# Reordering the last expert sets and moving the final norm's roots in a one-core transformer layer

## The chip, the cores and the metric

The kernel runs on one core of a Trainium2 chip. The metric is the device time of one execution in microseconds. TensorE (PE) multiplies, VectorE (DVE) and ScalarE (ACT) do elementwise work, GpSimd (POOL) issues the gathers and does small elementwise work, SyncE (SP) issues plain transfers. Each engine runs its own instructions in program order and waits for others by semaphores.

## The reference

One layer over 256 latent tokens of width 2048: an adaLN-modulated RMSNorm, a mixer (mLSTM and differential attention), a gated residual, and then the part that matters here, a PEER block (each token and head retrieves its best 16 of 16384 single-neuron experts), a second gated residual and a final RMSNorm:

```
def block(args):
    hx, ix, gx = args
    act = jax.nn.gelu(jnp.einsum('td,ted->te', hx, expert_u[ix]), approximate=False)
    return jnp.einsum('te,ted->td', (gx * act), expert_v[ix])
...
x = x + g2 * peer(...)
return rmsnorm(x, final_norm_w)      # x * rsqrt(mean(x*x) + EPS) * w
```

## The kernel before, in words

The 256 tokens are two tiles of 128 (tile 0 and tile 1). Everything up to the second einsum is left as it is by the change; what follows concerns the end, where gathered rows of expert_v are multiplied into the output.

**Blocks and items.** Lists of experts are cut into blocks of 128 rows. For each block POOL issues two gathers on its software queue, in this order: `ag` (gates and activations, L1548 to L1554, 128 columns for a block of a set, 256 for one of a whole tile, 512 for a block that serves both tiles) and `vraw` (128 rows of expert_v, 2048 floats each, 1 MB, L1528). `ITEMS` (L83) is the written-out order of the work. An item is one of:

- a *set*: four blocks of one tile, one for each group of 32 tokens. Each matmul is 128 rows by 32 tokens; 16 instructions in all (four blocks by four column chunks `c` of 512).
- a *pair set* (`PAIRS`): four blocks, each serving 32 tokens of tile 0 and 32 of tile 1, so 32 instructions: first all of tile 0, then all of tile 1.
- a *block of a whole tile* or of both tiles: raw rows are split by ACT (`hi`, L1559) and DVE (`lo`, L1561) into two float32r halves and multiplied in three passes, 12 matmuls for each tile that it serves.

In `ITEMS` of before the four pair sets are spread among the blocks of whole and both tiles; behind the fourth pair set come four such blocks and then three sets: `SETS[0][5]` (tile 0), `SETS[1][4]` and `SETS[1][5]` (tile 1). The last twelve blocks are therefore sets.

**Buffers.** `stage_rows` takes row buffers from a ring of six tiles of two rows each (L1510). A gather of `vraw` thus reuses the buffer of the block twelve before it, and has to wait until the matmuls (or splits) that read that block and its neighbour in the two-row tile are through. `fetch` (L1595) issues gathers up to this depth.

**The end** (L1794 on). `v_groups(t, item, parts, cs, last)` (L1620) multiplies an item into tile t's four accumulators `v`, chunk by chunk. `residual(t, c)` (L1797) multiplies the accumulator by the gate `g2` into `yf`, adds to `x` (both DVE), and squares with a sum on ACT into `s4`. For tile 1 and c < 2, POOL multiplies `x` by the final weight `fw` at L1804. `finish_tile(t)` (L1806) sums `s4`, makes the inverse root in `rstd` (DVE L208, then POOL's power L210), scales the four chunks by root and weight (DVE L1816; for tile 1, c < 2, ACT L1814) and stores them, on ACT's queue for c < 2 and on SP's for the rest. `item_weights` makes the 32-column weights `w` of an item on DVE (L1579) from its `ag`. Instructions marked `line` (DVE) and gathers keep the order in which the program writes them; the scheduler places others.

In before, tile 0 ends with the third item from the end; its residual is written in two halves around the weights of the last item, and its `finish_tile` follows the multiplications of the last item but one.

Of the kernel before, what the change touches and what calls it, by code (L numbers as in the profile page):

```python
# [19 lines left out]
F32 = mybir.dt.float32  # L20
# [5 lines left out]
AF = mybir.ActivationFunctionType  # L26
OP = mybir.AluOpType
# [4 lines left out]
P = 128  # L32
D = 2048
# [3 lines left out]
EPS = 1e-6  # L37
# [19 lines left out]
CAPS = (6,) * 8 + (8, 8, 16) + (1,) * 16  # L57
GOES = {0: ((4, EARLY), (1, LATER), (1, N_LIST)), 4: ((4, EARLY), (2, N_LIST))}
BASE = tuple(sum(CAPS[:i]) for i in range(len(CAPS)))
BOTH, PAIR, DENSE = 10, 11, 27  # L60
# [4 lines left out]
def group(kind, t):  # L65
    return kind % 4 if kind < 8 else ((kind - PAIR) % 4 + t * ((kind - PAIR) // 4)) % 4
# [7 lines left out]
def spread(*groups):  # L74
    return [x for _, _, x in sorted(((i + 0.5) / len(g), j, x) for j, g in enumerate(groups) for i, x in enumerate(g))]
# [4 lines left out]
SETS = [[[(4 * t + j, i) for j in range(4)] for i in range(6)] for t in range(2)]  # L80
SOON = [SETS[0][0], SETS[1][0], SETS[0][1], SETS[1][1]] + SETS[0][2:5]
PAIRS = [[(PAIR + 4 * d + g, 0) for g in range(4)] for d in range(4)]
ITEMS = SETS[1][2:4] + [[(DENSE, i)] for i in range(N_LIST, P)] + spread(  # L83
    PAIRS, [[(BOTH, i)] for i in range(CAPS[BOTH])], [[(8 + n % 2, n // 2)] for n in range(16)]) + [
    SETS[0][5], SETS[1][4], SETS[1][5]]


def build(tc, a, dump=None):
    nc = tc.nc
# [3 lines left out]
    def mp_(*args, **kw):  # L93
        tc.keep_in_program_order(mm(*args, **kw))  # L94
# [21 lines left out]
    def load(src, pool, bufs, queue=nc.sync):  # L116
        r = pool.tile([P, 1024], F32, name="raw", tag="raw", bufs=bufs)
        d = queue.dma_start(r, src)  # L118
        if by_four[0]:
            tc.keep_in_program_order(d)  # L120
        return r
# [7 lines left out]
    def line(i):  # L129
        if in_line[0]:  # L130
            tc.keep_in_program_order(i)
# [74 lines left out]
    def rstd(pool, ss, n, w, name):  # L206
        v = pool.tile([P, w], F32, name=name + "v", bufs=1)
        nc.vector.tensor_scalar(v, ss, 1.0 / n, EPS, op0=OP.mult, op1=OP.add)  # L208
        r = pool.tile([P, w], F32, name=name, bufs=1)
        nc.gpsimd.tensor_tensor(r, v, mhalf[:, :w], op=OP.pow)  # L210
        return r
# [221 lines left out]
    for k in range(KT):  # L433
# [7 lines left out]
        for kp in range(4):  # L441
            w = load(a["w_mod1"][k, kp], stx, MOD_BUFS)
# [661 lines left out]
    for k in range(KT):  # L1104
        x = rp.tile([P, T], F32, name="xk", tag="xk", bufs=3)
# [3 lines left out]
                                       op0=OP.add, op1=OP.subtract)  # L1109
# [388 lines left out]
    n = P - N_LIST + 1  # L1498
# [105 lines left out]
    def item_weights(n):  # L1604
        return [(raw, weights_of(kind, ins)) for (kind, _), (raw, ins) in
                zip(ITEMS[n], [fetched.pop(0) for _ in ITEMS[n]])]

    coming = []
# [11 lines left out]
    def v_groups(t, item, parts, cs=range(4), first=False, last=False, into=None):  # L1620
        for c in cs:
            for (kind, _), (raw, ins) in zip(item, parts):
                q = 32 * group(kind, t)
                mp_((into or out_acc[t][c])[q:q + 32, :], lhsT=ins[t], rhs=raw[:, c * 512:(c + 1) * 512],
                    start=first, stop=last, skip_group_check=True)


    x1 = [[None] * 4 for _ in range(2)]
# [75 lines left out]
    for i1 in range(0, P, 2):  # L1704
# [3 lines left out]
        act = act_tail if i1 == N_LIST else gm.tile([P, 2, T], F32, name="act", tag="act", bufs=2)  # L1708
        u_pair(act, pace)
        if i1 == N_LIST:  # L1710
            fetch(0)
            parts = item_weights(0)
        nc.scalar.activation(act, act, AF.Gelu)
        if i1 < N_LIST:
            rows = ag_dram[P + i1 * P:P + (i1 + 2) * P].rearrange("(i p) (t c) -> p i t c", p=P, t=2)
# [51 lines left out]
    with tc.If(rest > 0):  # L1767
        with tc.For_i(0, N_LIST, 1) as i:
            col_ = av.tile([P, 1], F32, name="ocol", bufs=1)
            nc.sync.dma_start(col_, over_dram[:, bass.ds(i, 1)])  # L1770
            for t in range(2):
# [3 lines left out]
                w = ag[:, :, 0]  # L1775
# [13 lines left out]
    N_LAST = len(ITEMS) - 3  # L1789
# [3 lines left out]

    fn = tc.alloc_tile_pool(name="fn", bufs=1, reuse_waits="tile")  # L1794
    s4 = fn.tile([P, 2, 5], F32, name="s4")

    def residual(t, c):  # L1797
        x = x1[t][c]
        y = gm.tile([P, 2, T], F32, name="yf", tag="act", bufs=2).rearrange("p a b -> p (a b)")
        line(nc.vector.tensor_tensor(y, out_acc[t][c], g2[c], op=OP.mult))  # L1800
        line(nc.vector.tensor_tensor(x, x, y, op=OP.add))  # L1801
        nc.scalar.activation(y, x, AF.Square, accum_out=s4[:, t, c:c + 1])  # L1802
        if t and c < 2:
            nc.gpsimd.tensor_tensor(x, x, fw[c // 2][:, c % 2 * 512:c % 2 * 512 + 512], op=OP.mult)  # L1804

    def finish_tile(t):  # L1806
        line(nc.vector.reduce_sum(s4[:, t, 4:5], s4[:, t, 0:4], axis=AX.X))
        r = rstd(fn, s4[:, t, 4:5], D, 1, f"rf{t}")
        rows = a["out"][t * P:(t + 1) * P, :]
        for c in (2, 0, 3, 1):  # L1810
            w = slice(c * 512, (c + 1) * 512)
            x = x1[t][c]
            if t and c < 2:
                nc.scalar.activation(x, x, AF.Copy, scale=r)  # L1814
            else:
                line(nc.vector.scalar_tensor_tensor(x, x, r, fw[c // 2][:, c % 2 * 512:c % 2 * 512 + 512],  # L1816
                                                    op0=OP.mult, op1=OP.mult))
            (nc.scalar if c < 2 else nc.sync).dma_start(rows[:, w], x)


    fnw = a["final_norm_w"]
    fw = [stg.tile([P, 1024], F32, name="fw", tag="raw", bufs=3) for _ in range(2)]
# [1 line left out]
        nc.sync.dma_start(fw[i], bass.AP(tensor=fnw.tensor, offset=fnw.offset + i * 1024, ap=[[0, P], [1, 1024]]))  # L1824
    fetch(N_LAST)
    coming.append(item_weights(N_LAST + 1))
    v_groups(0, ITEMS[N_LAST], coming.pop(0), last=True)
    for c in range(2):
        residual(0, c)
    coming.append(item_weights(N_LAST + 2))  # L1830
    for c in range(2, 4):
        residual(0, c)
    v_groups(1, ITEMS[N_LAST + 1], coming.pop(0))
    finish_tile(0)
    last = coming.pop()
    for c in range(4):
        v_groups(1, ITEMS[N_LAST + 2], last, (c,), last=True)
        residual(1, c)
    finish_tile(1)
    for p in (fn, vex, *v_pools, av, res, gates, vst, tkr, gm, stg, cst, dr):  # L1840
        p.release()

# [68 lines left out]
```

## Time and profile before

| what | us |
|---|---|
| median of 3 runs | 2252.41 |
| lowest and highest | 2245.99, 2253.37 |
| the profiled execution | 2240.84 |
| its span in the profile | 2239.1 |
| PE busy in the span | 2146.8 (96%) |
| DVE, ACT, POOL busy | 1536.1, 1022.1, 784.5 |

A timeline row reads: start and duration in us, engine, line, operation, output <- input, shapes, how many, and in brackets the idle time of that engine before it with what ended it. A row of windows gives, for a stretch of the span, each engine's busy time with its count, the clock granted to TensorE, the DMA engines' mean busy share and what they moved. Line numbers are those of the kernel before.

### The profile page before, as it was taken

The page shows a single profiled execution, that of the slowest core. Times are in us where ns is not written, and L with a number is a line of the kernel's source. Part 1 is how long each engine was busy: PE and PEld are TensorE (multiplying, and loading weights), DVE is VectorE, ACT ScalarE, POOL GpSimd, SP SyncE. Part 2 cuts the span into 40 slices and gives each one's busy share as a digit, 9 for nine tenths or more (in the row PEclk, how much of TensorE's full clock was granted, in tenths as well). Part 3 has the DMA queues.
Part 4 walks back from the last instruction along what each step waited for, and adds up shares of the span by engine and source line. Part 5 has one row for each costly group of instructions (what it writes and reads, how often), then busy time and mean ns, then how long its engine had stood idle before and what let it go on. Part 6 is the DMA issues. An engine that isn't in the chain of part 4 may idle for free. (4 is left out here: it accounts for less than half of the span.)

```text
span 2239.1 us, 37163 instructions
## 1 busy us (share of the span) xinstructions
PE 2146.8 (96%) x14098; PEld 1860.9 (83%) x14098; DVE 1536.1 (69%) x2781; ACT 1022.1 (46%) x1634; POOL 784.5 (35%) x799
## 2 busy tenths in 40 slices
PE   6999999999999999998999999998999999999996
PEld 3668998999899899987998888897888877786773
DVE  3438794566987786855679967777989644544664
ACT  3222232224465854444444678883446333333552
POOL 2122210225554321000223667781221323416763
PEclk9999999999999999999999999999999999999998
DMA  9958883776654678875556568888665798989995
GB/s 379 368 172 310 317 298 96 272 260 195 166 167 131 191 252 279 284 251 179 183 170 193 187 187 236 227 221 235 210 201 183 296 331 332 356 327 380 413 406 226
DMA packets 235845, 563.63 MB, mean 252 GB/s; under 512 B 85218, under 2 KB 118803, under 8 KB 222096
## 3 DMA queue, kind: packets, MB, share of 16 engines
q1 hardware_dynamic: 155328, 339.34, 46.1%
q0 software_dynamic: 45488, 204.33, 25.2%
q10 hardware_dynamic: 34848, 17.57, 2.7%
q8 instruction: 111, 1.82, 0.3%
q14 instruction: 70, 0.57, 0.1%
HBM read 516.99 MB, written 38.93 MB: 248 GB/s over the span
## 5 line engine op out<-in xcount | busy, mean ns | idle before, releaser
L140 ACT CAST hi<-raw 128x1024 fp32r<-128x1024 f32 x528 | 553.2, 1049 | 849.5 <-PE acc L300 275.3
L143 DVE TENSOR_TENSOR lo<-raw,hi 128x1024 fp32r<-128x1024 f32 x476 | 602.4, 1269 | 376.5 <-ACT hi L140 341.3
L94 PE MATMUL s<-h,hi 128*128 128x512 f32 x2048 | 529.1, 400 | 14.5 <-ACT hi L140 13.7
L94 PEld LDWEIGHTS s<-h,hi 128*128 128x128 f32 x2048 | 369.6, 190 | 93.4 <-ACT hi L140 19.3
L300 PE MATMUL acc<-hL,hi 128*128 128x256 f32 x2048 | 333.5, 284 | 0.0
L94 PEld LDWEIGHTS s<-h,lo 128*128 128x128 f32 x2048 | 280.3, 191 | 30.0 <-DVE lo L143 5.5
L300 PEld LDWEIGHTS acc<-hL,hi 128*128 128x128 f32 x2048 | 292.6, 192 | 1.8 <-ACT kA L677 0.3
L94 PE MATMUL s<-h,lo 128*128 128x256 f32 x2048 | 287.1, 283 | 6.9 <-DVE lo L143 3.8
L143 POOL TENSOR_TENSOR lo<-raw,hi 128x1024 fp32r<-128x1024 f32 x52 | 133.6, 2570 | 305.2 <-ACT hi L140 256.7
L300 PE MATMUL acc<-hL,lo 128*128 128x256 f32 x1024 | 175.7, 284 | 0.9 <-DVE lo L143 0.9
L533 DVE SCALAR_TENSOR_TENSOR raw<-raw,cr 128x1024 f32<-128x1024 f32 x128 | 156.3, 1234 | 21.3 <-DMA raw<-w_mod 17.3
L118 POOL DMA_DIRECT2D raw<-w_mod x128 | 67.9, 530 | 289.9 <-DVE raw L533 276.4
L1261 POOL TENSOR_SCALAR o<-iota,i1T,gT 128x128 f32<-128x128 f32 x128 | 147.5, 1160 | 56.4 <-PE g L94 27.9
L1532 POOL DMA_INDIRECT vraw<-expert_v,idxV x96 | 101.5, 1057 | 167.5 <-PE v L94 83.5
L300 PEld LDWEIGHTS acc<-hL,lo 128*128 128x128 f32 x1024 | 150.0, 192 | 2.2 <-DVE lo L143 1.3
L1532 POOL DMA_INDIRECT ag<-ag_dram,idxG x96 | 109.9, 1145 | 79.7 <-DMA ag_dram<-act 37.4
L1561 DVE TENSOR_TENSOR lo<-vraw,hi 128x1024 fp32r<-128x1024 f32 x68 | 82.9, 1225 | 68.4 <-ACT hi L1559 68.2
L300 PE MATMUL acc<-hC,hi 128*128 128x256 f32 x512 | 124.7, 283 | 0.0
L1244 DVE TENSOR_REDUCE act<-s 128x256 f32<-128x512 f32 x126 | 86.1, 684 | 51.0 <-PE s L94 47.4
L94 PE MATMUL v<-hi,l 128*128 128x512 f32 x416 | 114.5, 397 | 0.1
L1559 ACT CAST hi<-vraw 128x1024 fp32r<-128x1024 f32 x68 | 70.8, 1049 | 79.7 <-PE v L94 62.7
L300 PEld LDWEIGHTS acc<-hC,hi 128*128 128x128 f32 x512 | 98.3, 192 | 0.0
(440 smaller groups left out, 3313.4 us busy)
## 6 DMA issues: line engine op xcount, KB each, us to landing
raw<-expert_u SPq DMA_DIRECT2D x256, 512.0 KB, 4.2
raw<-w_in SPq DMA_DIRECT2D x176, 512.0 KB, 4.5
raw<-w_mod POOLq DMA_DIRECT2D x128, 512.0 KB, 5.5
raw<-w_mod SPq DMA_DIRECT2D x64, 512.0 KB, 8.6
raw<-w_out SPq DMA_DIRECT2D x32, 512.0 KB, 4.3
raw<-w_pq SPq DMA_DIRECT2D x32, 512.0 KB, 3.4
ag_dram<-gates SPq DMA_DIRECT2D x32, 512.0 KB, 6.2
ag_dram<-act ACTq DMA_DIRECT2D x126, 128.0 KB, 4.6
```

Of the source, the lines that this page charges most:

```text
L94: tc.keep_in_program_order(mm(*args, **kw))
L118: d = queue.dma_start(r, src)
L140: nc.scalar.copy(h, r)
L143: (nc.vector if shared[0] else nc.gpsimd).tensor_tensor(l, r, h.bitcast(F32), op=OP.subtract)
L300: mm(acc[c][:, g * T:(g + 1) * T], lhsT=hl[sb][:, k2 * 512 + c * P:k2 * 512 + (c + 1) * P], rhs=rhs(sa, g, k), start=first and k2 == 0 and ...
L533: product = nc.vector.scalar_tensor_tensor(r, r, 1.0, cr, op0=OP.mult, op1=OP.mult, accum_out=part[:, h, i:i + 1])
L1244: line(nc.vector.reduce_sum(act[:, e], ps.rearrange("p s t -> p t s"), axis=AX.X))
L1261: (nc.gpsimd if i % 2 else nc.vector).tensor_scalar(o2[:, i], iota, cols[:, i:i + 1], factor[:, i:i + 1], op0=OP.is_equal, op1=OP.mult)
L1532: tc.keep_in_program_order(nc.gpsimd.indirect_dma_start(out=out, out_offset=None, in_=src, in_offset=bass.IndirectOffsetOnAxis(ap=idx[:, b ...
L1559: nc.scalar.copy(h, raw)
L1561: nc.vector.tensor_tensor(l, raw, h.bitcast(F32), op=OP.subtract)
```

## The change

It does four things. In `ITEMS` the fourth pair set and `SETS[0][5]` change places: the set takes the pair set's place among the items, and the pair set is third from the end, so that it is the last item of tile 0. The inverse root is made by ACT (`Sqrt`, with `eps` as bias tile) and DVE (`reciprocal`) instead of DVE and POOL; a `Sqrt` on `eps` into `first` stands ahead of it, behind ACT's last split. POOL's two multiplications by `fw` (L1804) become two on DVE (L1852 in the kernel after), written behind tile 1's last residual. And the order at the end is written anew: tile 0's residual in one piece and its scaling behind the weights of the last item; all four stores of tile 0 on SP; tile 1's chunks 0, 1 scaled and stored by ACT in turn with 2, 3 by DVE and SP.

```
 ITEMS = SETS[1][2:4] + [[(DENSE, i)] for i in range(N_LIST, P)] + spread(
-    PAIRS, [[(BOTH, i)] for i in range(CAPS[BOTH])], [[(8 + n % 2, n // 2)] for n in range(16)]) + [
-    SETS[0][5], SETS[1][4], SETS[1][5]]
+    PAIRS[:3] + [SETS[0][5]], [[(BOTH, i)] for i in range(CAPS[BOTH])], [[(8 + n % 2, n // 2)] for n in range(16)]) + [
+    PAIRS[3], SETS[1][4], SETS[1][5]]
...
+    eps = fn.tile([P, 1], F32, name="eps")
+    nc.vector.memset(eps, EPS)
...
+    on_act(nc.scalar.activation(first, eps, AF.Sqrt))
...
-        nc.scalar.activation(y, x, AF.Square, accum_out=s4[:, t, c:c + 1])
-        if t and c < 2:
-            nc.gpsimd.tensor_tensor(x, x, fw[c // 2][:, c % 2 * 512:c % 2 * 512 + 512], op=OP.mult)
+        on_act(nc.scalar.activation(y, x, AF.Square, accum_out=s4[:, t, c:c + 1]))
...
-        r = rstd(fn, s4[:, t, 4:5], D, 1, f"rf{t}")
...
+        r = fn.tile([P, 1], F32, name=f"rf{t}")
+        on_act(nc.scalar.activation(r, s4[:, t, 4:5], AF.Sqrt, bias=eps, scale=1.0 / D))
+        line(nc.vector.reciprocal(r, r))
+        return r
...
-    v_groups(0, ITEMS[N_LAST], coming.pop(0), last=True)
-    for c in range(2):
+    parts = coming.pop(0)
+    v_groups(0, ITEMS[N_LAST], parts, last=True)
+    v_groups(1, ITEMS[N_LAST], parts)
+    for c in range(4):
         residual(0, c)
     coming.append(item_weights(N_LAST + 2))
-    for c in range(2, 4):
-        residual(0, c)
     v_groups(1, ITEMS[N_LAST + 1], coming.pop(0))
-    finish_tile(0)
+    r = root(0)
+    for c in range(4):
+        scaled(0, c, r)
     last = coming.pop()
     for c in range(4):
         v_groups(1, ITEMS[N_LAST + 2], last, (c,), last=True)
         residual(1, c)
-    finish_tile(1)
+    for c in range(2):
+        line(nc.vector.tensor_tensor(x1[1][c], x1[1][c], fw_of(c), op=OP.mult))
+    r = root(1)
+    for c in range(2):
+        scaled(1, c, r, act=True)
+        scaled(1, c + 2, r)
```

What moves on the engines is shown at three places. The first is POOL's queue where the fourth pair set's gathers stood. Before:

```order
L1532 DMA ag_21962<-ag_dram_83,idxG_10953 128x512
L1532 DMA vraw_21964<-expert_v,idxV_10952 128x2048
L1532 DMA ag_21966<-ag_dram_83,idxG_10953 128x512
L1532 DMA vraw_21964<-expert_v,idxV_10952 128x2048
L1532 DMA ag_21969<-ag_dram_83,idxG_10953 128x512
L1532 DMA vraw_21971<-expert_v,idxV_10952 128x2048
L1532 DMA ag_21973<-ag_dram_83,idxG_10953 128x512
```

After, at the same place:

```order
L1532 DMA ag_21962<-ag_dram_83,idxG_10953 128x128
L1532 DMA vraw_21964<-expert_v,idxV_10952 128x2048
L1532 DMA ag_21966<-ag_dram_83,idxG_10953 128x128
L1532 DMA vraw_21964<-expert_v,idxV_10952 128x2048
L1532 DMA ag_21969<-ag_dram_83,idxG_10953 128x128
L1532 DMA vraw_21971<-expert_v,idxV_10952 128x2048
L1532 DMA ag_21973<-ag_dram_83,idxG_10953 128x128
```

The gathers of gates shrink from 512 to 128 columns here; sixteen rows of the order further on, at `ag_22200`, four of them grow from 128 to 512. The gathers of rows stay as they are. POOL's four operations behind the last gather are gone.

The second is DVE's queue around tile 0's end (`v_184..` are tile 0's accumulators, `v_206..` tile 1's). Before:

```order
1891 L1801 TENSOR_TENSOR x_18692<-x_18692,yf 128x512
1892 L1579 TENSOR_TENSOR w_22536<-ag 128x32
1893 L1579 TENSOR_TENSOR w_22538<-ag 128x32
1894 L1579 TENSOR_TENSOR w_22540<-ag 128x32
1895 L1579 TENSOR_TENSOR w_22542<-ag 128x32
1896 L1800 TENSOR_TENSOR yf<-v_18449,g_2_18910 128x512
1897 L1801 TENSOR_TENSOR x_18693<-x_18693,yf 128x512
1898 L1800 TENSOR_TENSOR yf<-v_18450,g_3_18912 128x512
1899 L1801 TENSOR_TENSOR x1m<-x1m,yf 128x512
1900 L1807 TENSOR_REDUCE s_22492<-s_22492 128x1
1901 L208 TENSOR_SCALAR rf0v<-s_22492 128x1
1902 L1816 SCALAR_TENSOR_TENSOR x_18693<-x_18693,rf_22571,fw 128x512
```

After:

```order
1893 L1808 TENSOR_TENSOR yf<-v_18450,g_3_18912 128x512
1894 L1809 TENSOR_TENSOR x1m<-x1m,yf 128x512
1895 L1579 TENSOR_TENSOR w_22548<-ag 128x32
1896 L1579 TENSOR_TENSOR w_22550<-ag 128x32
1897 L1579 TENSOR_TENSOR w_22552<-ag 128x32
1898 L1579 TENSOR_TENSOR w_22554<-ag 128x32
1899 L1816 TENSOR_REDUCE s_22476<-s_22476 128x1
1900 L1819 RECIPROCAL rf_22573<-rf_22573 128x1
1901 L1827 SCALAR_TENSOR_TENSOR x_18691<-x_18691,rf_22573,fw 128x512
```

Tile 0's residual now stands wholly ahead of the last item's weights; its sum, root and scaling stand behind them, and tile 1's residual behind those, as before.

The third is ACT's queue at the end. After:

```order
996 L1559 CAST hi<-vraw 128x1024 x3
997 L1803 ACT_TABLE_LOAD
998 L1803 ACTIVATE first<-eps 128x1
999 L1810 ACTIVATE yf,s_22476<-x_18691 128x512
...
1007 L1810 ACTIVATE yf,s_22476<-x1m 128x512
1008 L1818 ACTIVATE rf_22619<-s_22476,eps 128x1
1009 L1825 ACTIVATE x_20691<-x_20691,rf_22619 128x512
1010 L1828 DMA out<-x_20691 128x512
1011 L1825 ACTIVATE x_20692<-x_20692,rf_22619 128x512
1012 L1828 DMA out<-x_20692 128x512
```

One load of activation tables stands behind the last split and none after it; the two stores now stand between and behind the two scalings, where before both stood behind. One further instruction has moved far: the scheduler puts the memset of `eps` on DVE between L1100 and L1106, in the norm ahead of the PEER block, where it waits for PE and for transfers on the hardware and software queues.

More of the change, by code (lines that the diff above doesn't have):

```diff
@@ L1795, in build, with on_act @@
     s4 = fn.tile([P, 2, 5], F32, name="s4")
+    eps = fn.tile([P, 1], F32, name="eps")
+    nc.vector.memset(eps, EPS)
+    def on_act(i):
+        tc.keep_in_program_order(i)
+    first = fn.tile([P, 1], F32, name="first")
+    on_act(nc.scalar.activation(first, eps, AF.Sqrt))
     def residual(t, c):
@@ L1801, in residual, with fw_of, root, scaled @@
         line(nc.vector.tensor_tensor(x, x, y, op=OP.add))
-        nc.scalar.activation(y, x, AF.Square, accum_out=s4[:, t, c:c + 1])
-        if t and c < 2:
-            nc.gpsimd.tensor_tensor(x, x, fw[c // 2][:, c % 2 * 512:c % 2 * 512 + 512], op=OP.mult)
-    def finish_tile(t):
+        on_act(nc.scalar.activation(y, x, AF.Square, accum_out=s4[:, t, c:c + 1]))
+    def fw_of(c):
+        return fw[c // 2][:, c % 2 * 512:c % 2 * 512 + 512]
+    def root(t):
         line(nc.vector.reduce_sum(s4[:, t, 4:5], s4[:, t, 0:4], axis=AX.X))
-        r = rstd(fn, s4[:, t, 4:5], D, 1, f"rf{t}")
[L1809 to L1818, printed above, removed]
+        r = fn.tile([P, 1], F32, name=f"rf{t}")
+        on_act(nc.scalar.activation(r, s4[:, t, 4:5], AF.Sqrt, bias=eps, scale=1.0 / D))
+        line(nc.vector.reciprocal(r, r))
+        return r
+    def scaled(t, c, r, act=False):
+        x = x1[t][c]
+        if act:
+            on_act(nc.scalar.activation(x, x, AF.Copy, scale=r))
+        else:
+            line(nc.vector.scalar_tensor_tensor(x, x, r, fw_of(c), op0=OP.mult, op1=OP.mult))
+        (nc.scalar if act else nc.sync).dma_start(a["out"][t * P:(t + 1) * P, c * 512:(c + 1) * 512], x)
     fnw = a["final_norm_w"]
```

## Prediction

> **What bounds the kernel now.** I read the page's span first, then the chain of waits, then the end's windows and timeline. The chain of waits is PE's matmuls for the whole of the items, and then something else:
>
> ```profile
> span 2239.1 us, 37163 instructions
> ...
> 2042.81 152.24 PE v L94 x784
> ...
> 2208.64 0.97 POOL vraw L1532
> 2209.60 8.99 issue
> ```
>
> From 2195 us on the chain runs through POOL's gathers, and the 8.99 us of "issue" behind the last one is no work of an engine: the last gathers are in flight there. So two stages count: the items, bound by PE, and the end, bound by the last eight gathers and what follows them. The windows show how the second begins (columns: PE, PEld, DVE, ACT, POOL busy, clock, DMA share, GB/s):
>
> ```profile
> 2184.00:2186.00 2.00, 2.00 (x24) 0.56 (x20) 1.63 (x4) 0.30 (x1) 0.51 (x1) 1.00 1.03 406
> 2186.00:2188.00 2.00, 2.00 (x24) 0.65 (x20) 0.00 (x0) 0.00 (x0) 0.00 (x0) 1.00 0.63 256
> 2188.00:2190.00 2.00, 2.00 (x16) 0.82 (x9) 0.00 (x0) 0.00 (x0) 0.47 (x1) 1.00 0.02 6
> 2190.00:2192.00 2.00, 2.00 (x10) 1.64 (x9) 0.00 (x0) 0.14 (x1) 1.42 (x2) 1.00 0.53 98
> 2192.00:2194.00 2.00, 2.00 (x11) 1.59 (x10) 1.05 (x1) 1.11 (x2) 1.67 (x2) 1.00 0.91 365
> ```
>
> The DMA engines are full, then lose 0.37 + 0.98 + 0.47 of three 2 us windows, some 3.6 us, and fill again. The timelines of PE and POOL say why:
>
> ```profile
> 2182.17 7.07 PE L94 MATMUL v<-vraw,w 128*32 128x512 f32 x64
> ...
> 2189.53 0.94 POOL L1532 DMA_INDIRECT vraw<-expert_v,idxV  x1 [5.02 <-PE v L94]
> ...
> 2206.16 8.15 PE L94 MATMUL v<-vraw,w 128*32 128x512 f32 x70
> 2207.38 0.95 POOL L1532 DMA_INDIRECT ag<-ag_dram,idxG  x1 [0.30 <-issue]
> 2208.64 0.97 POOL L1532 DMA_INDIRECT vraw<-expert_v,idxV  x1 [0.30 <-issue]
> 2214.52 0.19 DVE L1579 TENSOR_TENSOR w<-ag 128x32 f32<-128x32 f32 x1 [3.61 <-DMA ag<-ag_dram,idxG]
> 2217.05 3.59 PE L94 MATMUL v<-vraw,w 128*32 128x512 f32 x26 [2.73 <-DMA vraw<-expert_v,idxV]
> ```
>
> The 7.07 us are the fourth pair set: 32 instructions, recorded as 64. The gather that starts eight blocks from the end needs the buffer of the pair set's first blocks, and goes 0.36 us behind 2189.24. From there the gathers follow one another without a pause to the last, whose gates reach DVE at 2214.52 and whose rows reach PE at 2217.05. Behind that stands one chain on DVE:
>
> ```profile
> 2219.26 1.42 DVE L1816 SCALAR_TENSOR_TENSOR x<-x,rf,fw 128x512 f32<-128x512 f32 x2 [0.70 <-POOL rf L210]
> 2221.91 0.68 DVE L1800 TENSOR_TENSOR yf<-v,g 128x512 f32<-128x512 f32 x1
> 2222.63 0.69 DVE L1801 TENSOR_TENSOR x<-x,yf 128x512 f32<-128x512 f32 x1
> 2223.24 0.68 DVE L1800 TENSOR_TENSOR yf<-v,g 128x512 f32<-128x512 f32 x1
> 2224.22 3.24 POOL L1804 TENSOR_TENSOR x<-x,fw 128x512 f32<-128x512 f32 x2 [4.99 <-ACT yf L1802]
> 2225.28 1.04 DVE L1801 TENSOR_TENSOR x<-x,yf 128x512 f32<-128x512 f32 x1
> 2226.96 1.04 DVE L1801 TENSOR_TENSOR x1m<-x1m,yf 128x512 f32<-128x512 f32 x1
> 2228.85 0.16 DVE L1807 TENSOR_REDUCE s<-s 128x1 f32<-128x4 f32 x1 [0.85 <-ACT yf L1802]
> 2229.27 0.56 POOL L210 TENSOR_TENSOR rf<-rf1v,mhalf 128x1 f32<-128x1 f32 x1 [1.82 <-DVE rf1v L208]
> 2229.87 1.33 ACT L1814 ACTIVATE x<-x,rf 128x512 f32<-128x512 f32 x2 [1.05 <-POOL rf L210]
> 2231.31 0.33 SPq L1818 DMA_DIRECT2D out<-x1m  x1
> ```
>
> Tile 0's second half of the residual and its scaling occupy DVE from 2214.52 to 2221.9, though PE has tile 1's first chunk ready near 2218; tile 1's residual, root and scaling follow. The scaling of tile 1 starts at 2229.87, and 9.2 us of stores and closing lie behind it. My sum is for that start.
>
> **The change part by part.**
>
> *Set for pair set among the items.* PE reads the buffers that the gather waits for in 16 instructions instead of 32: 7.07 / 2 = 3.5 us sooner, so that gather goes at 2186.0. Would the DMA engines be free? The gates of four blocks shrink from 512 to 128 columns, 4 x 128 x 384 x 4 bytes = 0.79 MB less at 400 GB/s, 2 us; the same 2 us come back with the pair set's gates eight blocks later, still ahead of this gather. The windows show full DMA from there on, so the queue drains where it did, near 2187. A gather's data starts some 1.3 us behind its issue (2189.53 to where the window 2190 to 2192 is half busy), so at 2187.4. The gap of 3.6 us closes to about 0.5, and the rest of the chain of gathers is unchanged. The last gates land 3.5 us earlier, at 2211.0, and the last rows at 2213.55. Bounds: 0 if the heavier gates hold the queue to 2190, 3.6 if the gap closes wholly. I take 3.5, since the row of the wait names PE.
>
> *Pair set third from the end.* PE gets the 3.5 us back before the last two sets, so it comes to the last set when it did: 64 of the 70 records behind 2206.16 are 7.07 us, 2213.23. That was idle time then (2.73 us); now PE meets the rows as they land, and nothing is lost. A first chunk takes 1.21 us from its first matmul to DVE's reading it:
>
> ```profile
> 2207.37 0.69 DVE L1800 TENSOR_TENSOR yf<-v,g 128x512 f32<-128x512 f32 x1 [4.24 <-PE v L94]
> ```
>
> So tile 1's residual can't start before 2214.45.
>
> *Tile 0's residual in one piece.* The pair set's tile 0 comes at 2206.16 - 3.5 = 2202.7. Its first chunk is read at 2203.9, and four chunks at 1.33 us (2221.91 to 2223.24 is one) end at 2209.3. Everything here lies beside PE and the gathers: cost nothing. Were the cover gone, it would be the 2.7 us of two chunks that before stood behind 2214.52. What is late next is the new wait in this queue: the weights of the last item stand ahead of tile 0's sum, and wait for the last gates until 2211.0.
>
> *Tile 0's scaling.* Weights 0.2, sum 0.16, root and inverse on other engines (next part, 0.75 from the sum's start), four scalings as between 2219.26 and 2221.91, 2.65: 2211.0 + 0.2 + 0.05 + 0.75 + 2.65 = 2214.65. That is later than PE's 2214.45 and sets the start of tile 1's residual: 2214.65 instead of 2221.91, 7.26 us earlier. Its four stores on SP, one behind the other, end long before tile 1's.
>
> *Roots on ACT and DVE.* The nearest rows for a short ACT operation and a reciprocal:
>
> ```profile
> L817 DVE RECIPROCAL z<-z 128x2 f32<-128x2 f32 x16 | 2.5, 161 | 7.8 <-ACT pr L810 7.7
> L765 ACT ACTIVATE le<-le 128x2 f32<-128x2 f32 x1 | 0.2, 203 | 0.0
> L1713 ACT ACT_TABLE_LOAD x3 | 3.8, 1283 | 0.1
> 2208.83 0.63 ACT L1802 ACTIVATE yf<-x 128x512 f32<-128x512 f32 x1 [7.57 <-DVE x L1801]
> ```
>
> From the sum's start: 0.16, a hop of 0.09, 0.20, a hop of 0.06, 0.16, a hop of 0.08: 0.75, against 1.02 before (2228.85 to 2229.87). Gain 0.27; bounds 0 (each hop twice as long) and 0.4. The table load of 1.28 us lies in the 7.57 us that ACT idles there; without that cover it would be 1.28. The Trainium skill, "ScalarE: Activation LUTs", section "What ACT_TABLE_LOAD costs", has a drain of 1.38 us come on top, 2.66 us for a switch; the idle time hides either, and the sum is the same by both.
>
> *Products by fw on DVE.* Without POOL beside it two of DVE's adds take 0.69 instead of 1.04: the four residuals last 5.4 instead of 6.1 us. Two products of 0.62 each follow, while ACT squares the last chunk, which before kept the sum waiting 0.85 us anyway. The sum starts 4 x 1.33 + 2 x 0.62 + 0.05 = 6.6 us behind the first residual, against 2228.85 - 2221.91 = 6.94. Gain 0.34; bounds 0 and 0.7.
>
> *Stores.* ACT now issues its first store (0.33) between its two scalings, so the second store goes later than before by that issue and a hop, up to 0.45. Four stores are 1 MB:
>
> ```profile
> 2230.00:2232.00 2.00, 0.00 (x0) 0.00 (x0) 1.28 (x2) 1.20 (x2) 0.00 (x0) 0.50 0.27 99
> 2232.00:2234.00 2.00, 0.00 (x0) 0.00 (x0) 0.00 (x0) 0.00 (x0) 0.00 (x0) 0.50 1.03 378
> ```
>
> The transfers, not the issues, fill that stretch, so I take 0.15; bounds 0 and 0.45.
>
> *The memset of eps* stands now between L1100 and L1106, where DVE idles:
>
> ```profile
> 1061.75 1.27 DVE L1106 SCALAR_TENSOR_TENSOR xk<-x1T,mod,m 128x256 f32<-128x256 f32 x3 [1.18 <-PE m L1101]
> ```
>
> It is one column and disappears in the 1.18 us, if what it waits for is over.
>
> Sum: 7.26 + 0.34 + 0.27 - 0.15 = 7.7 us. On the profiled execution's 2240.84 that gives 2233.1. The runs' median is 2252.41, 11.6 above that execution; the gain is at the end and not in what differs between runs, so I subtract it there: 2244.7, 0.34% faster. About 0.3% is what a measurement of this kernel can tell from no change, so the forecast lies at that edge.
>
> **The rivals.**
>
> *The gathers come no earlier* (queue held by the heavier gates, or POOL's own issue late). Then the gates land at 2214.52 as before, and only tile 0's residual is out of the way: start at 2214.52 + 0.2 + 0.05 + 0.75 + 2.65 = 2218.2, 3.7 earlier; with the other terms 4.2 us: 2248.2, no change that can be told. For it speaks that the DMA engines are full for tens of microseconds before the gap; against it the gap itself.
>
> *More table loads than one.* If the square or the scaled copy needed other tables than the root, two loads of 1.28 us would stand on the chain, before and behind the second root: 7.7 - 2.6 = 5.1 us, 2247.3. The order has one load behind the last split and none after, which speaks against it. (The Trainium skill, "ScalarE: Activation LUTs", section "Table sets: the hidden batching unit", has one expensive function to a set, and a switch for a function that is not in it.)
>
> *The memset holds DVE* in the norm ahead of the experts. Its place in the queue is ahead of L1106, and ACT's and PE's next work waits for that line. If what it waits for ends x us behind 1060.6, the kernel loses x - 1.2 us; from x = 8.9 it is slower than before, and with x = 16, as after a slow transfer, by 7 us: 2259. Against it: the buffer that it reuses must be from an earlier stage, since none that is then live may be overwritten.
>
> **How the numbers follow.** Full shift 0.70; no earlier gathers 0.17; more loads 0.05; memset 0.04; the rest, something not named, 0.04. Runs of before differ by 7 us among three, so a true gain of 0.34% shows as more than 0.3% about two times in three, and one of 0.19% one time in seven. Faster: 0.70 x 0.68 + 0.17 x 0.15 + 0.03 = 0.53. Slower: the memset and a little of the rest, 0.06. Same: 0.41. The range goes from the profiled execution less the whole gain, 2233, to the highest run less 4.2, 2249, and one more for bounds: 2233 to 2250.
>
> **What would show it.** In the profile after: the gap of the DMA share near 2187 gone or under 1 us; the gather behind the set at 2186 with a wait for PE near 1.5 us instead of 5.02; PE without an idle stretch from the items to its last matmul; DVE's last weights at 2211; tile 1's first residual near 2214.7, right behind tile 0's fourth scaling; no add of 1.04; tile 1's scaling near 2222. I am wrong if the gap stays, if the last weights still come at 2214, if a table load appears behind the first root, or if L1106 waits longer than 1.2 us.

## The result and the profile after

| | median us | runs | lowest, highest |
|---|---|---|---|
| before | 2249.14 | 8 | 2245.99, 2253.83 |
| after | 2237.19 | 8 | 2233.17, 2243.25 |

The ratio is 0.995, with a 95% interval of 0.9936 to 0.9964: 8 to 14 us faster, 11 in the middle. In a later series, with 12 runs of after and 35 of before on one chip, it was 0.996 (0.9944 to 0.9976): 5 to 13 us, 9 in the middle. The forecast was 7.7 us, so the sign was right and the size somewhat small. As a time it was 2244.7 us, in a range of 2233 to 2250, and 2237.19 was measured. Of the 7.5 us between the two, 3.3 lie in the base: before's median was 2252.41 over three runs and is 2249.14 over eight.

The profiled execution of after took 2233.17 us, with a span of 2231.4. Its span is 7.7 us shorter than before's, but that equality is chance. The stage ahead of the change differs from execution to execution, and in after's it has a hole in its chain of waits (start, length, what) that after's second execution, further down, does not have in its chain:

```profile
2037.71 50.99 PE v L94 x244
2088.70 3.62 issue
2092.32 117.30 PE v L94 x588
```

So all traces are read from one fixed place, called so from here on: the first matmul of the item at the fourth pair set's place, 2182.17 in before and 2184.06 in after. From there to the span's end before took 56.9 us and after 47.3: 9.6 us, of which the stage ahead gave 1.9 back.

The timelines of PE and POOL in after, which answer to before's 7.07 us set and 5.02 us wait:

```profile
2184.06 3.64 PE L94 MATMUL v<-vraw,w 128*32 128x512 f32 x32
...
2187.97 1.01 POOL L1532 DMA_INDIRECT vraw<-expert_v,idxV  x1 [0.32 <-PE v L94]
...
2204.62 14.63 PE L94 MATMUL v<-vraw,w 128*32 128x512 f32 x128
```

The gather behind the set goes 3.91 us behind the set's first matmul, where before's went 7.36 behind. PE's last three sets are one piece, without the 2.73 us of waiting. The windows show that the DMA engines no longer pause (share in the last column but one; before had 0.63, 0.02 and 0.53 from 2186 to 2192):

```profile
2186.00:2188.00 2.00, 2.00 (x18) 0.58 (x11) 2.00 (x4) 0.33 (x1) 1.38 (x3) 1.00 1.01 412
2188.00:2190.00 2.00, 2.00 (x10) 1.64 (x9) 0.17 (x1) 0.00 (x0) 1.70 (x2) 1.00 1.04 428
2190.00:2192.00 2.00, 2.00 (x10) 1.59 (x10) 0.65 (x1) 1.25 (x2) 1.39 (x3) 1.00 1.03 401
```

Then DVE's timeline in after:

```profile
2208.19 0.69 DVE L1808 TENSOR_TENSOR yf<-v,g 128x512 f32<-128x512 f32 x1 [6.18 <-PE v L94]
...
2213.64 0.49 DVE L1579 TENSOR_TENSOR w<-ag 128x32 f32<-128x32 f32 x4
2214.57 0.16 DVE L1816 TENSOR_REDUCE s<-s 128x1 f32<-128x4 f32 x1 [0.44 <-ACT yf L1810]
2215.09 0.16 DVE L1819 RECIPROCAL rf<-rf 128x1 f32<-128x1 f32 x1 [0.36 <-ACT rf L1818]
2215.29 2.08 DVE L1827 SCALAR_TENSOR_TENSOR x<-x,rf,fw 128x512 f32<-128x512 f32 x3
2217.28 0.75 DVE L1827 SCALAR_TENSOR_TENSOR x1m<-x1m,rf,fw 128x512 f32<-128x512 f32 x1
2217.94 0.69 DVE L1808 TENSOR_TENSOR yf<-v,g 128x512 f32<-128x512 f32 x1
...
2223.26 1.28 DVE L1852 TENSOR_TENSOR x<-x,fw 128x512 f32<-128x512 f32 x2
2224.46 0.15 DVE L1816 TENSOR_REDUCE s<-s 128x1 f32<-128x4 f32 x1
2224.97 0.16 DVE L1819 RECIPROCAL rf<-rf 128x1 f32<-128x1 f32 x1 [0.36 <-ACT rf L1818]
2225.17 0.75 DVE L1827 SCALAR_TENSOR_TENSOR x<-x,rf,fw 128x512 f32<-128x512 f32 x1
```

Tile 1's residual starts 33.88 behind the fixed place, instead of 39.74 in before. Two things stand out. Tile 0's first chunk is read 3.57 us behind its set's first matmul (2204.62), not 1.21, and holds DVE up: the last weights don't wait for gates, they wait for DVE. And from the start of tile 1's scaling (2225.17) to the span's end it is 6.2 us, where before had 9.2 and the prediction took 9.2 as given.

The waits of SP's queue at the end show the second (engine, line and what it waited for; us in total, times, the longest). In before:

```profile
SPq L1907 <- PEq L1907: 3.7, 2, 3.1
SPq L1907 <- DMA out<-x1m: 2.9, 1, 2.9
```

and in after:

```profile
SPq L1924 <- DMA out<-x: 2.8, 1, 2.8
SPq L1924 <- PEq L1924: 0.7, 2, 0.6
```

L1907 and L1924 are where the program ends. SP waits about as long for the last store in both; behind it the longest wait for the other engines is 3.1 us in before and 0.6 in after. The stores don't explain that: in before the DMA engines move nothing from 2235 to 2239 (shares of 0.00), and the span ends at 2239.1. The profile doesn't say which engine comes to the end last. The one whose late work differs between the two kernels is POOL: in before its power runs from 2229.27 to 2229.83 (shown in the prediction), in after its last work is the issue of a gather at 2207.11.

**Theory.** The gain has three parts: gathers that go 3.5 us sooner because PE frees the buffers sooner; an order on DVE in which tile 0's residual no longer stands behind the last gates; and POOL, whose end comes some 9 us behind its last elementwise operation and outlasted the stores. **Rivals:** the shorter closing was chance; the swap is worth nothing without the new order, or the order nothing without the swap; the late first chunk belongs to the changed order.

### The profile page after: what moved, and what is told of

Its sections match the earlier page's. It is cut to its first block, busy times and chain, and to the rows that moved or that the text cites. A ratio compares the mean times of both kernels' runs of the same rounds, so it can differ in the third digit from the quotient of the medians.

```text
span 2231.4 us, 37166 instructions
## 1 busy us (share of the span) xinstructions
PE 2142.7 (96%) x14098; PEld 1859.3 (83%) x14098; DVE 1534.7 (69%) x2784; ACT 1023.8 (46%) x1638; POOL 789.4 (35%) x795
## 5 line engine op out<-in xcount | busy, mean ns | idle before, releaser
L1532 POOL DMA_INDIRECT ag<-ag_dram,idxG x96 | 115.3, 1201 | 75.0 <-DMA ag_dram<-act 35.8
L94 PEld LDWEIGHTS v<-hi,l 128*128 128x128 f32 x416 | 79.0, 191 | 29.7 <-issue 11.0
```

Of the source, the lines that this page charges most:

```text
L1532: tc.keep_in_program_order(nc.gpsimd.indirect_dma_start(out=out, out_offset=None, in_=src, in_offset=bass.IndirectOffsetOnAxis(ap=idx[:, b ...
```

## The experiments

All places are in us behind the fixed place, from one profiled execution of each kernel. "Last weights" is the start of DVE's last L1579 (in after, of its last four, which stand in one row). "Closing" in the text is the time from the start of tile 1's scaling to the span's end. Each ratio is to runs of before on the same chip; the swap alone, no swap, the roots and products alone and the late POOL operation ran on one chip, the other experiments and after again on another.

| kernel | last weights | tile 1's residual | tile 1's scaling | span's end | ratio to before (95%) |
|---|---|---|---|---|---|
| before | 32.35 | 39.74 | 47.70 | 56.9 | |
| after | 29.58 | 33.88 | 41.11 | 47.3 | 0.995 (0.9936 to 0.9964) |
| after again | 27.96 | 32.08 | 39.31 | 45.6 | 0.996 (0.9944 to 0.9976) |
| swap alone | 28.02 | 35.42 | 43.37 | 52.6 | 0.9993 (0.9981 to 1.0006) |
| no swap | 31.14 | 34.83 | 42.05 | 48.3 | 0.9976 (0.9962 to 0.999) |
| roots and products alone | 31.25 | 38.32 | 45.55 | 51.8 | 0.9978 (0.9966 to 0.9989) |
| POOL operation late | 28.14 | 32.08 | 39.31 | 49.4 | 0.9974 (0.9961 to 0.9988) |
| POOL operation early | 27.99 | 32.08 | 39.31 | 45.6 | 0.9955 (0.9939 to 0.997) |
| products on POOL | 28.37 | 32.62 | 40.28 | 47.4 | 0.9958 (0.9944 to 0.9973) |
| no early table load | 28.95 | 32.55 | 39.78 | 46.0 | 0.995 (0.9934 to 0.9967) |
| second table load | 29.13 | 32.74 | 40.79 | 47.1 | 0.9956 (0.9938 to 0.9974) |
| stores by SP | 28.47 | 32.08 | 39.31 | 45.6 | 0.9955 (0.9938 to 0.9972) |

The runs of one kernel on one chip differ by up to 18 us, so a ratio holds to 3 or 4 us. The places hold to a tenth where no transfer sets them; the last weights, which wait for gathers, differ by 1.2 us between executions of the same order. So the places carry the argument.

### The swap alone

```
 # before
-    PAIRS, ...) + [SETS[0][5], SETS[1][4], SETS[1][5]]
+    PAIRS[:3] + [SETS[0][5]], ...) + [PAIRS[3], SETS[1][4], SETS[1][5]]
...
-    v_groups(0, ITEMS[N_LAST], coming.pop(0), last=True)
+    parts = coming.pop(0)
+    v_groups(0, ITEMS[N_LAST], parts, last=True)
+    v_groups(1, ITEMS[N_LAST], parts)
```

> Before with one thing changed: the fourth pair set stands third from the end and tile 0's set 5 in its place, so PE's set there has 16 instructions instead of 32; DVE's order at the end, the roots and the products stay as before. All numbers from the first matmul of the item in the pair set's place, since the stage ahead of it differs by microseconds between executions; from there to the span's end it is 56.9 us in before and 47.3 in after. Theory (the gathers go 3.5 us sooner because PE frees the buffers sooner, and all behind moves with them): last gates at +28.6 instead of +32.3, tile 1's residual at +36.0 instead of +39.7, scaling start to span end still 9.2, stretch 53.2, a gain of 3.7 us. Rival (the order on DVE is what counts, and the swap alone gives its time back to a later wait): gates earlier, but tile 1's residual within 1 us of +39.7, gain 0 to 1.

Measured: 52.6, residual at 35.42, closing 9.2. On POOL's and DVE's timelines:

```profile
2186.09 3.64 PE L94 MATMUL v<-vraw,w 128*32 128x512 f32 x32
```

```profile
2190.00 0.94 POOL L1532 DMA_INDIRECT vraw<-expert_v,idxV  x1 [1.69 <-PE v L94]
...
2214.11 0.19 DVE L1579 TENSOR_TENSOR w<-ag 128x32 f32<-128x32 f32 x1 [2.91 <-DMA ag<-ag_dram,idxG]
2214.22 0.68 DVE L1800 TENSOR_TENSOR yf<-v,g 128x512 f32<-128x512 f32 x1
...
2221.51 0.69 DVE L1800 TENSOR_TENSOR yf<-v,g 128x512 f32<-128x512 f32 x1
```

The wait for PE is 1.69 us, the "near 1.5" of the prediction, and the gates still end a wait of DVE (2.91), with tile 0's second half behind them: all moves by what the gates move, 4.3 us. In the trace the theory holds, and the rival, a residual that stays within 1 us of 39.7, is out. Over the runs the gain can't be told from none (1.6 us, interval -1.3 to 4.3), and 4.3 is at the edge of that. One reason is in the next two runs.

### All but the swap

```
 # after
-    PAIRS[:3] + [SETS[0][5]], ...) + [PAIRS[3], SETS[1][4], SETS[1][5]]
+    PAIRS, ...) + [SETS[0][5], SETS[1][4], SETS[1][5]]
...
-    v_groups(1, ITEMS[N_LAST], parts)
```

> After without the swap: the order of the items is that of before (the fourth pair set amid the items, tile 0's set 5 third from the end), all else of the change stays. Theory: the DMA gap of 3.6 us behind the pair set and POOL's wait of 5.0 for PE come back, last gates at +32.3; but tile 0's residual is out of the way of the gates, so tile 1's residual starts near +36.0 (gates + 0.25 + 0.75 + 2.65), against +39.7 in before and +33.9 in after; scaling to span end 6.2; stretch 49.5, a gain of 7.4 us over before and 2.2 us slower than after. Rival (the swap is needed for any of it): residual at +39 or later, and only the closing's 3 us are left.

Measured: 48.3, residual at 34.83, closing 6.2. POOL shows the old wait for PE again, as said, and DVE's row gives the residual's start:

```profile
2191.97 0.94 POOL L1532 DMA_INDIRECT vraw<-expert_v,idxV  x1 [5.00 <-PE v L94]
...
2219.44 0.69 DVE L1808 TENSOR_TENSOR yf<-v,g 128x512 f32<-128x512 f32 x1
```

The residual comes 1.2 us sooner than expected, and the last weights are 1.21 sooner than in before (31.14, not 32.35) with the same order of gathers. The kernel with roots and products alone has 31.25. In all three POOL issues the last gather 26.47 us behind the fixed place, so it is the landing that differs: before's own profile caught its last gates about 1.1 us late. With the swap that last issue stands at 23.02 to 23.05 in all nine traces that have it, 3.4 us sooner, and the gates come some 3.2 us sooner (31.2 to 28.0, the early ones of each order) rather than the 4.3 read against before's profile. In after's order 2.7 of that reach the end (48.3 against 45.6), and the whole change is worth some 10 us rather than 11.3. The rival, that the order is worth nothing without the swap, is out: against gates that are not late it moves the residual's start by 3.8 us (39.74 - 1.1 - 34.83), where the prediction's case of gathers that come no earlier had 3.7. Of these, 0.3 are tile 0's root: against the next kernel, which has the roots but not the order, it is 38.32 - 34.83 = 3.5.

### Roots on ACT and DVE, products on DVE, nothing else

```
 # before
...
+    on_act(nc.scalar.activation(first, eps, AF.Sqrt))
...
-        if t and c < 2:
-            nc.gpsimd.tensor_tensor(x, x, fw[...], op=OP.mult)
...
+        for c in range(2 * t):
+            line(nc.vector.tensor_tensor(x1[t][c], x1[t][c], fw[0][:, c * 512:c * 512 + 512], op=OP.mult))
...
-        r = rstd(fn, s4[:, t, 4:5], D, 1, f"rf{t}")
+        r = fn.tile([P, 1], F32, name=f"rf{t}")
+        on_act(nc.scalar.activation(r, s4[:, t, 4:5], AF.Sqrt, bias=eps, scale=1.0 / D))
+        line(nc.vector.reciprocal(r, r))
```

> Before with the roots on ACT and DVE and tile 1's two products on DVE, so that POOL has nothing behind its last gather; the items and DVE's order at the end as before. Theory: 0.3 us from the root, 0.4 us from the residual without POOL beside it, 3.0 us from the closing (6.2 instead of 9.2): stretch 53.2 instead of 56.9, a gain of 3.7 us with the start of tile 1's residual at +39.7 as before. Rival (the closing was chance): 9.2 again, a gain of 0.7 us.

Measured: 51.8, closing 6.3, the ratio 0.9978, 4.9 us (2.5 to 7.6). The rival is out: before's order and no POOL operation at the end give the short closing. The residual starts at 38.32, 1.42 sooner than in before: 1.1 for the gates, as above, and 0.3 for tile 0's root, which this expectation had left out.

### A POOL operation behind the last root

```
 # after, behind the last root
+    idle = fn.tile([P, 1], F32, name="idle")
+    nc.gpsimd.tensor_tensor(idle, r, mhalf[:, :1], op=OP.mult)
```

> After with one POOL operation more: a multiplication of 128 x 1 behind the last root, for which nobody waits. Theory (POOL's end comes 8.5 us behind its last elementwise operation, and the program's end waits for it): the operation ends near where before's power did, so scaling start to span end is 9.2 us instead of 6.2, all ahead of it unchanged, the stretch 50.3 instead of 47.3. Rival (the closing's 3 us have nothing to do with POOL): 6.2 and 47.3 as in after.

Measured: the residual's and the scaling's places as in after's second run (32.08, 39.31), and a closing of 10.1 instead of 6.3. SP's waits have the long one back:

```profile
SPq L1926 <- PEq L1926: 4.5, 2, 4.0
SPq L1926 <- DMA out<-x: 2.8, 1, 2.8
```

The closing is 0.9 longer than expected because the operation ended 0.81 behind the scaling's start, where before's power ended 0.04 ahead of it:

```profile
2218.25 0.76 POOL L1855 TENSOR_TENSOR idle<-rf,mhalf 128x1 f32<-128x1 f32 x1 [15.36 <-DVE rf L1819]
```

From its end, 2219.01, to the span's end at 2228.3 it is 9.29; from the power's end in before 2239.1 - 2229.83 = 9.27. One column that nobody reads costs the kernel 3.8 us.

### The same operation, early

```
 # after, behind tile 0's residual
+    idle = fn.tile([P, 1], F32, name="idle")
+    nc.gpsimd.tensor_tensor(idle, s4[:, 0, 0:1], mhalf[:, :1], op=OP.mult)
```

> After with one POOL multiplication of 128 x 1 more, as in the run with it behind the last root, but here behind the last gather, on tile 0's first partial sum; nobody waits for it. From the first matmul of the item in the pair set's place it is 45.5 us to the end where tile 0's first chunk is read 1.21 us behind its set's first matmul (the run with the late operation, 49.4, less the 3.9 that its closing was longer), and 47.3 where it is read late, as in after's own profile. Theory (the program's end waits until 9.3 us behind POOL's last elementwise operation): the operation ends near +25, so POOL is through at about +34, long before the stores; scaling start to span end stays 6.2, stretch 45.5 (47.3). Rival (any elementwise operation on POOL in this stage makes the end longer, wherever it stands): closing 9 or more, stretch 48.5 or more.

Measured: 45.6 and a closing of 6.25.

```profile
2205.97 0.54 POOL L1843 TENSOR_TENSOR idle<-s,mhalf 128x1 f32<-128x1 f32 x1
```

It ends at 2206.51, 21 us ahead of the span's end, and costs nothing. It is not that POOL is used, but how late.

### The products back on POOL

```
 # after
         on_act(nc.scalar.activation(y, x, AF.Square, accum_out=s4[:, t, c:c + 1]))
+        if t and c < 2:
+            nc.gpsimd.tensor_tensor(x, x, fw[...], op=OP.mult)
...
-    for c in range(2):
-        line(nc.vector.tensor_tensor(x1[1][c], x1[1][c], fw_of(c), op=OP.mult))
```

> After with tile 1's two products by the norm's weight back on POOL, behind the squares, where before has them; roots stay on ACT and DVE. Two terms are told apart. DVE beside POOL: two of the four adds take 1.04 instead of 0.69 and the sum stands 6.94 behind the start of tile 1's residual instead of 6.52, so scaling starts 0.42 later. The end: in before the second product ended 5.55 behind that start; theory (POOL's end comes 9.3 us behind its last elementwise operation of whatever size, with the last steps of the program) gives an end at 14.8 behind it, where the stores alone give 6.94 + 0.71 + 6.27 = 13.9: closing 7.2, stretch 32.1 + 14.8 = 46.9 against after's 45.6. Rival (the long end belongs to the power or to operations of one column): closing 6.3, stretch 46.0.

Measured, from POOL's and DVE's timelines:

```profile
2218.68 0.69 DVE L1808 TENSOR_TENSOR yf<-v,g 128x512 f32<-128x512 f32 x1 [0.69 <-PE v L94]
...
2220.99 3.24 POOL L1812 TENSOR_TENSOR x<-x,fw 128x512 f32<-128x512 f32 x2 [10.93 <-ACT yf L1810]
...
2222.06 1.04 DVE L1809 TENSOR_TENSOR x<-x,yf 128x512 f32<-128x512 f32 x1
...
2225.63 0.16 DVE L1818 TENSOR_REDUCE s<-s 128x1 f32<-128x4 f32 x1 [0.85 <-ACT yf L1810]
```

The sum stands 6.95 behind the residual's start (6.94 said), the products end 5.55 behind it at 2224.23, and the span ends 9.27 behind that, at 2233.5: the closing is 7.2. POOL's end follows its last elementwise operation at the same distance, for two of 512 columns as for one of one. The rival, that the long end belongs to the power or to operations of one column, is out. The stretch is 47.4 and not 46.9, because the residual itself starts at 32.62: PE's last three sets take 14.59 us here and not 13.94, and DVE waits for PE. So of after's gain the products on DVE are worth 0.4 for the quieter DVE and 0.9 for POOL's end, with the roots off POOL already.

### No early table load

```
 # after
-    first = fn.tile([P, 1], F32, name="first")
-    on_act(nc.scalar.activation(first, eps, AF.Sqrt))
```

> After without the early root of eps, so that ACT's table load stands directly before tile 0's root. ACT is free from the end of its last square of tile 0, 0.4 us ahead of tile 0's sum. Theory: the load is 1.28 us long and costs what that idle time and DVE's 0.4 us of waiting for PE don't cover: root 0.85 us later, tile 1's residual at +32.5 instead of +32.1, the stretch 0.5 us longer, 46.0 instead of 45.5 (where the first chunk is read late, DVE sets the start and it is 0.85: 48.2 instead of 47.3). If the load waits for the sum as the root does: +0.9 (+1.28). By the Trainium skill, ScalarE: Activation LUTs, section What ACT_TABLE_LOAD costs, a drain of 1.38 comes on top: root 2.2 later, stretch +1.85. Rival (the load is hidden wherever it stands, and the early root does nothing): 0.

Measured: 46.0, the 0.5 expected.

```profile
2212.17 0.19 ACT L1808 ACTIVATION_READ_ACCUMULATOR yf<-x1m 128x1 f32 x1
2212.38 1.28 ACT L1816 ACT_TABLE_LOAD   x1
2213.67 0.29 ACT L1816 ACTIVATE rf<-s,eps 128x1 f32<-128x1 f32 x1
```

The load follows the square at once, lasts 1.28 us, and the root follows at once: no drain beside it. But the number decides nothing here: in this execution the last weights came 1.0 us later than in after's second, and tile 0's sum only at 2213.42, 0.24 us ahead of the load's end. Gates and load ended together, and either alone would have given 32.55 within a tenth. The clean test is the next one.

### A second table load, on the path

```
 # after
     r = root(0)
+    on_act(nc.scalar.activation(first, eps, AF.Exp))
```

> After with an exponential of eps on ACT behind tile 0's root, whose result nobody reads: it brings one table load into ACT's 5.0 us of waiting for tile 1's residual, and a second directly before tile 1's root, which is the prediction's rival of more table loads than one. ACT is through with its last square 6.22 us behind the start of tile 1's residual, and the root starts at 6.70 in after's second profile. Theory (a load takes its 1.28 us and no more, and the one in the waiting time is free): root at 6.22 + 1.28 + 0.03 = 7.53, 0.83 later, stretch from the pair set's place to the end 46.4 instead of 45.6. By the Trainium skill, ScalarE: Activation LUTs, section What ACT_TABLE_LOAD costs, a drain of 1.38 comes on top: root 2.2 later, stretch 47.8. By the prediction's rival the whole 1.28 for each of two: 48.2.

Measured, on ACT's timeline from tile 0's root on:

```profile
2216.70 0.29 ACT L1818 ACTIVATE rf<-s,eps 128x1 f32<-128x1 f32 x1 [1.43 <-DVE s L1816]
2217.02 1.28 ACT L1845 ACT_TABLE_LOAD   x1
2218.31 0.20 ACT L1845 ACTIVATE first<-eps 128x1 f32<-128x1 f32 x1
2221.53 0.63 ACT L1810 ACTIVATE yf<-x 128x512 f32<-128x512 f32 x1 [3.02 <-DVE x L1809]
...
2226.26 1.28 ACT L1818 ACT_TABLE_LOAD   x1
2227.55 0.29 ACT L1818 ACTIVATE rf<-s,eps 128x1 f32<-128x1 f32 x1
```

Tile 1's residual starts at 2220.02, so the root stands 7.53 behind it: the theory's number, 0.83 later than without the load. The first load is hidden. The rest of the longer stretch (47.1) is the residual's start at 32.74, with late gates (29.13) and 14.71 us of PE's last sets, as with the products on POOL (14.59).

### The first store of tile 1 by SP

```
 # after, with a parameter by in scaled for the engine that issues the store
...
-    for c in range(2):
-        scaled(1, c, r, act=True)
-        scaled(1, c + 2, r)
+    scaled(1, 0, r, act=True, by=nc.sync)
+    scaled(1, 2, r)
+    scaled(1, 1, r, act=True)
+    scaled(1, 3, r)
```

> After with tile 1's first store issued by SP instead of ACT, so that ACT's second scaling follows its first without the issue of a store between them. In after that issue and a hop take 0.45 us, the second scaled copy starts 1.18 us behind the first, and its store is the last to be issued. Theory (the last store's issue sets the end): second scaling at 0.66 behind the first, its store issued 0.5 us earlier, closing 5.7 to 5.8 instead of 6.2, all ahead of it unchanged. Rival (the transfers or the engines' end set it): 6.2.

A miss: ACT's two scalings follow each other without a pause, and the closing is 6.25, as in after.

```profile
2228.25 1.33 ACT L1825 ACTIVATE x<-x,rf 128x512 f32<-128x512 f32 x2 [0.23 <-DVE rf L1819]
2229.61 0.35 ACTq L1828 DMA_DIRECT2D out<-x  x1
```

The second scaled copy is stored at 2229.61, 1.36 behind the scaling's start instead of 1.93 (2224.74 - 2222.81 in after's second run), and the last of the four issues ends at 2.04 (SP's) instead of 2.28; yet nothing is won. The first issue stands where it stood, 0.74 us behind the scaling's start (0.75 in after's second run), and the transfers that it starts fill the stretch: the DMA engines are full from 2230 to 2232 here (shares 1.03, 1.04) and from 2225 to 2227 there (1.05, 1.03). The windows behind have shares of 0.60 (from 2232) and 0.19 (from 2227), so by estimate the last transfer ends some 1.9 us ahead of the span's end in both.

### After again

> After itself on this chip, beside the single edits. Theory: the late reading of tile 0's first chunk in after's profile (3.57 us behind its set's first matmul) was that execution's own; here 1.21 as in the others, tile 1's residual at +32.1 and the stretch 45.5; median gain over before 11.4 us less what differs between chips, and clearly more than any single edit (1.6, 5.4 and 4.9 us for the swap alone, all but the swap, and the roots and products alone). Rival (the late reading belongs to the changed order): 3.57 again, +33.9, stretch 47.3, gain 9.6.

Measured: 45.6, the residual at 32.08, and on DVE's timeline

```profile
2205.28 0.69 DVE L1808 TENSOR_TENSOR yf<-v,g 128x512 f32<-128x512 f32 x1 [3.84 <-PE v L94]
...
2211.46 0.19 DVE L1579 TENSOR_TENSOR w<-ag 128x32 f32<-128x32 f32 x1 [0.47 <-DMA ag<-ag_dram,idxG]
...
2215.58 0.69 DVE L1808 TENSOR_TENSOR yf<-v,g 128x512 f32<-128x512 f32 x1 [0.56 <-PE v L94]
...
2222.81 0.75 DVE L1827 SCALAR_TENSOR_TENSOR x<-x,rf,fw 128x512 f32<-128x512 f32 x1
```

The first of these is 1.21 us behind its set's first matmul at 2204.07. All seven other runs with the swap have 1.21 to 1.22 too, so the 3.57 was that one execution's. What it was stays open. PE's weight loads come in fours there, 0.43 us apart, and then out of step (in after's own profile):

```profile
2207.22 0.13 PEld L94 LDWEIGHTS v<-vraw,w 128*32 128x32 f32 x4 [0.30 <-issue]
...
2208.53 0.11 PEld L94 LDWEIGHTS v<-vraw,w 128*32 128x32 f32 x1 [0.23 <-issue]
2208.96 0.11 PEld L94 LDWEIGHTS v<-vraw,w 128*32 128x32 f32 x1 [0.32 <-issue]
2209.59 0.19 PEld L94 LDWEIGHTS v<-vraw,w 128*32 128x32 f32 x7 [0.51 <-issue]
```

No version in the study beat after: the stores by SP and the early POOL operation end at the same 45.6.

## Why the prediction was right, step by step

**Set for pair set among the items: right.** Said: the gather 3.5 us sooner, the wait for PE near 1.5, the gap under 1 us. Measured: 3.45, a wait of 1.69 in all runs with the swap but after's own profile (0.32), and shares of 1.01 to 1.04, so no gap. The last gates were to come at 28.8 behind the fixed place; they came at 28.0 to 29.1 where they set the weights. One reading in the prediction is off: before's gather goes 0.29 us behind 2189.24, not 0.36. Nothing hangs on it.

**Pair set third from the end: right, with one thing not foreseen.** PE's idle time is gone. But the rows of the last block now land about when PE wants them, 30.5 behind the fixed place. By issue and time to landing they come at 30.3 to 30.5 in four traces with the swap, where PE's last three sets take 13.94 us, at 30.8 in one with 14.02, and at 31.3 to 31.5 in three, where the sets take 14.52 to 14.71, and tile 1's residual starts at 32.55 to 32.74 instead of 32.08 (in one of these three runs DVE waits 0.69 us for PE, in the other two late gates or the table load hold it about as long). So the gathers have no slack left, and the variation of their landing goes into the end.

**Tile 0's residual, tile 0's scaling: right in size, with the two waits the other way round.** The prediction had 1.21 us to the first chunk, DVE at 2214.65 and PE at 2214.45 for the start of tile 1's residual, that is 32.5 and 32.3, so DVE was to come last. Measured: 32.08, where DVE has waited 0.56 us for PE, since the gates landed at 28.0 and DVE was through at 31.5. The gain of the term is 7.66 instead of 7.26 (5.86 in the one execution with the late first chunk), or about 6.6 against a before whose gates are not late.

**Roots and products: right.** Sum to scaling 0.71 (0.75 said, 1.02 before), residual to sum 6.52 (6.6 said, 6.94 before). One table load, hidden in ACT's waiting. The rival of more loads was overpriced: a load on the path costs 0.83, since ACT is idle for 0.45 of it, and one in the waiting time costs nothing. The Trainium skill, "ScalarE: Activation LUTs", section "What ACT_TABLE_LOAD costs", would have 1.38 of drain on top; in the three places behind an ACT instruction with nothing else to wait for, ACT loses the 1.28 and some 0.04 around it. The measurement decides: 7.53 and not 8.9.

**Stores: nothing to be seen** of the 0.15. SP waits 2.8 us for the last of them, against 2.9 in before, and moving one of them to SP changes nothing. Against before itself the term can't be read, since POOL set the end there.

**The memset of eps: right.** L1106 waits 1.18 us for the same matmul as before.

**The closing: the term that was mis-sized.** "The scaling of tile 1 starts at 2229.87, and 9.2 us of stores and closing lie behind it. My sum is for that start." It took these 9.2 us for a constant of the kernel, while 3 of them were POOL's and went with its last elementwise operation: 6.3 in after. The hint was in the profile of before, in SP's 3.1 us of waiting for the other engines behind the last store. With it the sum of the prediction would have been 10.7.

The terms as measured in after's second run, against before's profile: 7.66 + 0.42 + 0.31 + 2.94 = 11.3 us; less the 1.1 us by which that profile's gates were late, 10.2. The ratios give 9 and 11.

## What to carry to other kernels

What stands behind the last store is part of the path: read the waits at the program's end, and let an engine whose end is slow be through with its elementwise work early. A pause of the DMA engines in front of the end can be closed by freeing the buffers that the next gather waits for; here the order of the items did that, with the gathers of rows left as they were. When executions differ by more than the gain, measure from one fixed instruction to the end, and profile the kernel twice before a single odd number is explained.

## What was not expected of the hardware

The span ended 9.27 to 9.29 us behind the end of POOL's last elementwise operation in all four kernels where the stores were through by then (before, the swap alone, the late operation, the products on POOL), whether that was a power or a product, one column or 512. Ended 21 us ahead of the span's end, the operation of one column cost nothing. What POOL does in that time the profile doesn't show. Whether a late gather has the same tail was not tried.
